# A two-layer encoder on one core: mask and maximum in one instruction, scaled queries, one sine product per rotation, a new TensorE order, first weights in halves

## The chip, the cores and the metric

The kernel runs on one core of a Trainium2 chip. The metric is the device time of one execution in microseconds; lower is better. The core has five engines that run their own instruction streams and wait for each other by semaphores: TensorE (PE in the profile; PEld is its weight load), VectorE (DVE), ScalarE (ACT), GpSimd (POOL) and SyncE (SP), which here does nothing but start DMA transfers. TensorE writes its results to PSUM, from where ACT and DVE take them.

## The reference

Input is x of 256 tokens by 1024, float32. There are two layers (DEPTH 2), each of three parts with a layer norm behind it:

```
x = layer_norm(ALPHA * x + 0.5 * swiglu(x, ffn1_w_in[l], ffn1_w_out[l]), ...)
mix = hybrid_mixer(x, cos, sin, mask, w_in[l], w_out[l], ...)
x = layer_norm(ALPHA * x + mix, ...)
x = layer_norm(ALPHA * x + 0.5 * swiglu(x, ffn2_w_in[l], ffn2_w_out[l]), ...)
```

`swiglu` is (silu(x Wg) * (x Wu)) W_out with a hidden width of 2816. The mixer projects x by one matrix into dq, dk, dv (512 columns each, 4 heads of two 64-wide halves), sq (512, 8 heads), sk and sv (128 each, 2 heads). The q and k parts are rotated (`t * cos + rot * sin`, where rot swaps the halves of each 64 columns and negates one). The first group is a differential attention, softmax(q1 k1) - lam * softmax(q2 k2), scores times 1/8, with a root-mean-square norm of each head. The second is attention in a window of 128 to either side, with a sink per head:

```
m = jnp.maximum(jnp.max(s, axis=-1, keepdims=True), sk)
e = jnp.exp(s - m)
p = e / (jnp.sum(e, axis=-1, keepdims=True) + jnp.exp(sk - m))
```

Both outputs side by side go through one output projection.

## The kernel before, in words

Every matrix product that needs float32 accuracy is made of three: a weight tile `raw` (128 by 1024 float32, 512 KB, by a DMA that SP starts) is split into `wh`, a cast on ACT (line 79), and `wl`, the rest, a subtraction on DVE (line 80). The activations lie in `xx`, hi and lo, transposed. A product is then hi x wh, hi x wl and lo x wh. There are 317 casts in all: 316 tiles, the first of them in two halves. `Weights._make` makes a tile, `get(i)` asks for tiles up to 8 ahead. `raw` has 5 buffers, `wh` and `wl` 9 each, so a cast can wait for the matmuls that used the buffer before. ACT and DVE are in-order: a cast that waits holds all behind it.

TensorE's order is the order in which the program is written (`manual_schedule`). The order on ACT, DVE and SP is made by a scheduler from priorities and its own estimate of times; `tc.high_priority` puts work ahead, and the splitting of weights stands 100 behind (`LATER`).

An FFN has a first part of 1024 columns, all 8 blocks k of the contraction for both token halves (`first`, tile `hb`, line 308), then 18 column tiles (`col`, tiles `hg` and `hu`, lines 340 and 342), then the second matrix (`step`, tile `acc`, line 390). The first FFN begins the program: its xx comes from `x_tr` by `load_xt`, in pieces of k (0:1, 1:2, 2:4, ...), between the first weight tiles. Nine matmuls on zeros (`wps`, line 162) run before the first real one.

The mixer is a list of steps, ORDER, for token blocks t of 128: `P nm t c` does c of the four parts of projection nm (tile `pj`, lines 455 to 457) and behind the last the rotation `rope_` on DVE (lines 470, 473, and 477 or 479); `X` transposes the second block of x; `T` transposes a rotated q or k (tile `tq`); `S d q` and `S s q` are the scores of two heads for query block q (tiles `sd` and `ss`, line 497) with the softmax on DVE and ACT; `A` transposes weights of the differential attention (`tpd`, line 570), `V` multiplies them by v (`od`) and normalises to `y`; `W` does the same for the windowed part (`tps`, `os`, line 614); `Y` transposes y into xx; `O t c` does c of the eight steps of the output projection (tile `ao`, line 678); `G` loads a norm's factors; `Z` transposes x for what follows.

In `swa_scores` a unit of two heads has two score tiles of 128 by 2 by 256. The mask is added to one half of each (line 539), the maximum is taken (line 540), line 543 scales it and takes the maximum with the sink, lines 546 and 547 make the arguments of exp, then follow the exps on ACT (line 554), sums, reciprocals and four multiplications (line 562).

Of the kernel before, what the change touches and what calls it, by code (L numbers as in the profile page):

```python
# [9 lines left out]
F32 = mybir.dt.float32  # L10
# [36 lines left out]
ORDER = """  # L47
P dk 0 1; P dq 0 2; P dk 0 2; X; P dq 0 1; P dq 1 1; P dk 0 1; P dv 0 2; P dk 1 2; P dq 0 1; P dv 1 1; P dq 1 2;
P dk 1 2; P dv 1 2; P dq 1 1; P dv 0 1; P dv 1 1; T dk 1; T dk 0; T dq 0; P sk 0 1; P dv 0 1; S d 0; P sq 0 1; T
dq 1; P sk 1 1; S d 0; P sk 0 1; P sk 1 3; P sq 0 1; A 0 0; T sk 1; P sk 0 1; S d 1; S d 1; P sk 0 1; P sq 0 2;  # L50
P sq 1 2; A 0 1; T sq 0; T sk 0; V 0; S s 0; P sq 1 1; A 1 1; A 1 0; P sq 1 1; S s 0; V 1; Y 0; G; T sq 1; O 0
2; S s 1; W 0 0; O 0 1; Y 1; W 0 1; W 0 2; O 0 1; S s 1; O 1 1; W 1 0; O 0 1; O 1 1; O 0 1; W 1 1; O 0 2; W 1 2;
O 1 4; Z; O 1 2
"""
# [38 lines left out]
def encoder_kernel(  # L93
# [84 lines left out]
    def load_x():  # L178
        for t in range(2):
# [18 lines left out]
    inv_t = cp.tile([P, 32], F32, name="inv_t")  # L198
    cos_t = cp.tile([P, 2, HD], F32, name="cos_t")
    sin_t = cp.tile([P, 2, HD], F32, name="sin_t")  # L200

    def rotary():
# [43 lines left out]
        dv.tensor_scalar(a, a, -1.0, math.pi / 2, ALU.mult, ALU.add)  # L246
        nc.scalar.activation(sin_t[:, :, 32:64], r, AF.Sin)
        nc.scalar.activation(cos_t[:, :, 0:32], a, AF.Sin)
        dv.tensor_copy(cos_t[:, :, 32:64], cos_t[:, :, 0:32])
        dv.tensor_scalar(sin_t[:, :, 0:32], sin_t[:, :, 32:64], -1.0, None, ALU.mult)  # L250

# [43 lines left out]
    def ffn(l, n, last=False):  # L295
# [4 lines left out]
        def first(ts, mid=None):  # L300

            hp = [[ps.tile([P, 512], F32, tag="b", name=f"hb_{nm}_{t}{s}") for s in range(2)] for t in ts]
            for k in range(KT):
                wh, wl = W.get(wi + k)
                for t, hb in zip(ts, hp):
                    for g, ww, e in ((0, wh, 0), (0, wl, 1), (1, wh, 2)):
                        for s in range(2):
                            mm(hb[s], xx[:, k, g, t, :], ww[:, 512 * s : 512 * s + 512],  # L308
                               start=(k == 0 and e == 0), stop=(k == KT - 1 and e == 2))
                if k == KT - 3 and mid is not None:  # L310
                    mid()
# [110 lines left out]
    def mixer(l):  # L422
# [38 lines left out]
        def rope_(pt, nh, t, nm, perm=False):  # L461
# [6 lines left out]
            m2v = m2[:, 0:w].rearrange("p (h d) -> p h d", d=HD)  # L468
            c = cos_t[:, t : t + 1, :].to_broadcast([P, nh, HD])
# [348 lines left out]
```

## Time and profile before

| what | value |
|---|---|
| median of three runs | 964.08 us (963.94 to 964.37) |
| the profiled execution's own time | 964.06 us |
| its span, first to last instruction | 962.2 us |
| PE busy | 947.0 us (98%) |
| DVE busy | 673.7 us (70%) |
| ACT busy | 509.4 us (53%) |
| mean granted TensorE clock | 0.997 |

The profile comes from one execution. Its own time is its span and about 1.9 us around it. Busy time of PE counts a matmul up to its modelled end, so matmuls overlap in the rows: a 128x512 matmul is shown with about 390 ns, while the next one starts after about 227. A wait of less than the overlap leaves no idle time in the rows, so start times say more than idle times.

### The profile page before, as it was taken

What the parts mean: (1) busy time and instruction counts of PE and PEld (TensorE: products, weight loads), DVE (VectorE), ACT (ScalarE), POOL (GpSimd) and SP (SyncE); (2) the same over time, 40 slices, a digit from 0 to 9 for tenths busy, and PEclk for the clock granted to TensorE, in tenths of its full rate; (3) what the DMA queues carried; (4) which work ended last, traced back from release to release, by engine and by line L of the source; (5) the groups of instructions that cost most, each with busy time, mean ns of one, the idle gap of its engine ahead of it and who ended that gap; (6) DMA issues with size and microseconds to landing.
All of it is one profiled execution on the core that took longest, in us unless ns stands there. A gap on an engine that the chain in (4) does not pass through costs nothing.

```text
span 962.2 us, 13695 instructions
## 1 busy us (share of the span) xinstructions
PE 947.0 (98%) x5087; PEld 801.8 (83%) x5087; DVE 673.7 (70%) x1099; ACT 509.4 (53%) x887; POOL 16.9 (2%) x27
## 2 busy tenths in 40 slices
PE   8999999999999999999999999999999999999997
PEld 6888888888778888888888888888887788888886
DVE  6887754589968776664587667547898787667534
ACT  5668553336755656543346555433576556555420
POOL 0000000000000000000000000000000000000000
PEclk9999999999999999999999999999999999999999
DMA  8886555366415755556376555563752276555511
GB/s 314 301 288 195 185 185 194 123 221 198 131 47 176 267 191 191 183 185 193 123 252 230 196 179 194 179 195 127 259 137 90 75 234 239 196 178 196 177 64 44
DMA packets 50946, 176.42 MB, mean 183 GB/s; under 512 B 6208, under 2 KB 8000, under 8 KB 50880
## 3 DMA queue, kind: packets, MB, share of 16 engines
q1 hardware_dynamic: 50880, 175.55, 55.6%
q8 instruction: 40, 0.66, 0.3%
q14 instruction: 26, 0.21, 0.1%
HBM read 174.48 MB, written 1.05 MB: 182 GB/s over the span
## 4 chain that ended last, share of the span: by engine, by line
PE 91%; DVE 5%; ACT 1%; issue 1%; DMA 0%; POOL 0%; SPq 0%; DVEq 0%; ACTq 0%
PE acc L390 25%; PE hg L340 14%; PE hu L340 14%; PE hb L308 9%; PE hu L342 7%; PE hg L342 7%; PE ao L678 4%; DVE wl L80 1%; PE tps L570 1%; PE os L614 1%; PE pj_dq L457 1%; PE pj_dv L457 1%; PE pj_dq L455 1%; PE pj_dv L456 1%; PE pj_dk L457 1%; PE pj_dv L455 1%
## 5 line engine op out<-in xcount | busy, mean ns | idle before, releaser
L80 DVE TENSOR_TENSOR wl<-raw,wh 128x1024 fp32r<-128x1024 f32 (+1 forms) x317 | 385.5, 1219 | 206.7 <-ACT wh L79 204.0
L79 ACT CAST wh<-raw 128x1024 fp32r<-128x1024 f32 (+1 forms) x317 | 332.1, 1050 | 330.7 <-PE acc L390 123.7
L390 PE MATMUL acc<-wh,g 128*128 128x512 f32 (+1 forms) x748 | 192.7, 377 | 0.0
L390 PEld LDWEIGHTS acc<-wh,g 128*128 128x128 f32 x748 | 136.0, 188 | 25.8
L340 PE MATMUL hg<-xx,wh 128*128 128x512 f32 x576 | 144.8, 393 | 0.0
L340 PE MATMUL hu<-xx,wh 128*128 128x512 f32 x576 | 144.2, 392 | 0.0
L340 PEld LDWEIGHTS hg<-xx,wh 128*128 128x128 f32 x576 | 103.6, 189 | 18.6
L340 PEld LDWEIGHTS hu<-xx,wh 128*128 128x128 f32 x576 | 103.6, 189 | 18.5
L390 PE MATMUL acc<-wl,g 128*128 128x512 f32 (+1 forms) x374 | 111.4, 377 | 0.0
L342 PEld LDWEIGHTS hg<-xx,wl 128*128 128x128 f32 x576 | 78.6, 190 | 5.7
L342 PEld LDWEIGHTS hu<-xx,wl 128*128 128x128 f32 x576 | 78.6, 190 | 5.6
L342 PE MATMUL hu<-xx,wl 128*128 128x256 f32 x576 | 80.3, 282 | 0.0
L342 PE MATMUL hg<-xx,wl 128*128 128x256 f32 x576 | 80.3, 282 | 0.0
L390 PEld LDWEIGHTS acc<-wl,g 128*128 128x128 f32 x374 | 68.9, 188 | 13.2
L308 PE MATMUL hb<-wh,xx 128*128 128x512 f32 x256 | 71.1, 395 | 1.0 <-ACT wh L79 1.0
L308 PEld LDWEIGHTS hb<-wh,xx 128*128 128x128 f32 x256 | 48.5, 191 | 11.7 <-ACT wh L79 1.8
L308 PE MATMUL hb<-wl,xx 128*128 128x512 f32 x128 | 40.4, 396 | 0.8 <-DVE wl L80 0.8
L678 PE MATMUL ao<-wh,xx 128*128 128x512 f32 x128 | 39.0, 406 | 1.8 <-DVE xx L270 1.0
L347 DVE TENSOR_TENSOR tl<-tl 128x256 f32<-128x256 f32 x72 | 30.6, 425 | 2.6 <-ACT tl L345 0.4
L349 ACT CAST g<-tl 128x256 fp32r<-128x256 f32 x72 | 28.9, 402 | 6.2 <-DVE tl L347 6.2
L350 DVE TENSOR_TENSOR g<-tl,g 128x256 fp32r<-128x256 f32 x72 | 30.1, 419 | 1.9 <-ACT g L349 1.9
L678 PEld LDWEIGHTS ao<-wh,xx 128*128 128x128 f32 x128 | 22.6, 188 | 9.6 <-issue 2.3
(182 smaller groups left out, 950.3 us busy)
## 6 DMA issues: line engine op xcount, KB each, us to landing
raw<-in_f_in_dram SPq DMA_DIRECT2D x144, 512.0 KB, 3.7
raw<-in_f_out_dram SPq DMA_DIRECT2D x88, 512.0 KB, 3.5
raw<-in_m_in_dram SPq DMA_DIRECT2D x36, 512.0 KB, 4.0
raw<-in_f_b_dram SPq DMA_DIRECT2D x31, 512.0 KB, 3.5
raw<-in_m_out_dram SPq DMA_DIRECT2D x8, 512.0 KB, 4.9
raw<-in_m_out_dram SPq DMA_DIRECT2D x16, 256.0 KB, 4.5
lng<-in_ln_g_dram SPq DMA_DIRECT2D x6, 512.0 KB, 5.5
lnb<-in_ln_b_dram SPq DMA_DIRECT2D x6, 512.0 KB, 6.1
```

What stands on the lines that cost most here:

```text
L79: nc.scalar.copy(wh[:, s], raw[:, s])
L80: nc.vector.tensor_tensor(wl[:, s], raw[:, s], wh[:, s].bitcast(F32), ALU.subtract)
L308: mm(hb[s], xx[:, k, g, t, :], ww[:, 512 * s : 512 * s + 512], start=(k == 0 and e == 0), stop=(k == KT - 1 and e == 2))
L340: mm(hs[s], wh[:, k * P : (k + 1) * P], xx[:, k], start=(k == 0), stop=False)
L342: mm(hs[s][:, 1, :], wl[:, k * P : (k + 1) * P], xx[:, k, 0], start=False, stop=(k == KT - 1))
L347: dv.tensor_tensor(gv, tl[:, 0], gv, ALU.mult)
L349: nc.scalar.copy(gs[q][:, jj, 0, :], gv)
L350: dv.tensor_tensor(gs[q][:, jj, 1, :], gv, gs[q][:, jj, 0, :].bitcast(F32), ALU.subtract)
L390: mm(a, g, ww[:, s], start=(k == 0 and e == 0), stop=(k == JT - 1 and e == 2))
L455: mm(o, xx[:, k, 0, t, :], wh[:, s], start=(k == 0), stop=False)
L457: mm(o, xx[:, k, 1, t, :], wh[:, s], start=False, stop=(k == KT - 1))
L678: mm(acc[t][h], xx[:, k, g, t, :], ww[:, s], start=(k == 0 and e == 0), stop=(k == KT - 1 and e == 2))
```

## The change

Five edits.

- First weights: the first three tiles (before: the first one) are loaded, cast and subtracted in halves of 512 columns, and without the lower priority; the first piece of x_tr is started by ACT in place of SP; for k below 3 the matmuls go by halves s, hi x wh for both token blocks, then lo x wh, then hi x wl.
- Mask and maximum: the mask is three blocks wide (a triangle, zeros, the other triangle), and one DVE instruction per head row of 256 adds it, starts the maximum from the sink and writes both. The lines that added the mask to halves, reduced and took the maximum with the sink are gone.
- Scale: cos and sin exist twice, one copy times 1/8, which the queries use. The exps lose their scale, the differential maximum is negated in the reduction, and its own multiplication by -1/8 goes.
- Rotation: one product with the sine over all 64 columns, reading the halves in reversed order, in place of two.
- The list ORDER is another one, and the scratch tile `jk` has one buffer in place of two.

```diff
-P dk 0 1; P dq 0 2; P dk 0 2; X; P dq 0 1; P dq 1 1; P dk 0 1; P dv 0 2; P dk 1 2; P dq 0 1; P dv 1 1; P dq 1 2;
+P dq 0 3; P dk 0 2; P dq 0 1; P dk 0 1; X; P dk 0 1; P dq 1 1; P dv 1 1; P dv 0 1; P dk 1 1; P dv 0 1; P dv 1 1;
...
-        n = 512 if i == 0 else 1024
+        n = 512 if i < 3 else 1024
...
-            with self.tc.high_priority(-LATER):
+            with self.tc.high_priority(0 if i < 3 else -LATER):
...
-        nc.sync.dma_start(xr, x_tr[:, :, k, :])
+        (nc.sync if k0 else nc.scalar).dma_start(xr, x_tr[:, :, k, :])
...
+        for tab in (cos_t, sin_t):
+            dv.tensor_scalar(tab[:, 0], tab[:, 1], SCALE, None, ALU.mult)
...
+                parts = ((0, wh, 0), (0, wl, 1), (1, wh, 2))
+                if wi + k < 3:
+                    todo = [(t, hb, parts[e], s) for s in range(2) for e in (0, 2, 1) for t, hb in zip(ts, hp)]
+                else:
+                    todo = [(t, hb, p, s) for t, hb in zip(ts, hp) for p in parts for s in range(2)]
...
-            for h in range(2):
-                sn = sin_t[:, t : t + 1, 32 * h : 32 * h + 32].to_broadcast([P, nh, 32])
-                dv.tensor_tensor(m2v[:, :, 32 * h : 32 * h + 32], src[:, :, 32 - 32 * h : 64 - 32 * h], sn, ALU.mult)
+            sn = sin_t[:, tab, t : t + 1, :].to_broadcast([P, nh, HD]).rearrange("p h (x d) -> p h x d", x=2)
+            dv.tensor_tensor(m2v.rearrange("p h (x d) -> p h x d", x=2),
+                             src.rearrange("p h (x d) -> p h x d", x=2)[:, :, ::-1, :], sn, ALU.mult)
...
-                    dv.tensor_reduce(mx[:, 2 * c : 2 * c + 2], sc[c], AX.X, ALU.max)
-                dv.tensor_scalar(mx, mx, -SCALE, None, ALU.mult)
+                    dv.tensor_reduce(mx[:, 2 * c : 2 * c + 2], sc[c], AX.X, ALU.max, negate=True)
...
-                    mb = mask[:, qt : qt + 1, :].to_broadcast([P, 2, P])
-                    dv.tensor_tensor(sc[v][:, :, ob], sc[v][:, :, ob], mb, ALU.add)
-                    dv.tensor_reduce(mx[:, 2 * v : 2 * v + 2], sc[v], AX.X, ALU.max)
+                    for i in range(2):
+                        q = 2 * v + i
+                        dv.tensor_tensor_reduce(sc[v][:, i, :], sc[v][:, i, :], mask[:, (1 - qt) * P : (3 - qt) * P], 1.0, sk[:, v, i : i + 1],
+                                                ALU.add, ALU.max, mx[:, q : q + 1])
...
-                dv.scalar_tensor_tensor(mx2, mx2, SCALE, sk, ALU.mult, ALU.max)
```

How the instructions stand. TensorE at the start, behind the nine matmuls on zeros, all twelve matmuls of the first k: before, where `hb_00` and `hb_01` are the two column halves of token block 0, `hb_10` and `hb_11` those of block 1, `wh_99` and `wl_100` the parts of the first tile:

```order
L308 MATMUL hb_00_195<-wh_99,xx 128x512
L308 MATMUL hb_01_196<-wh_99,xx 128x512
L308 MATMUL hb_00_195<-wl_100,xx 128x512
L308 MATMUL hb_01_196<-wl_100,xx 128x512
L308 MATMUL hb_00_195<-wh_99,xx 128x512
L308 MATMUL hb_01_196<-wh_99,xx 128x512
L308 MATMUL hb_10_197<-wh_99,xx 128x512
```

and now:

```order
L318 MATMUL hb_00_201<-wh_99,xx 128x512
L318 MATMUL hb_10_203<-wh_99,xx 128x512
L318 MATMUL hb_00_201<-wh_99,xx 128x512
L318 MATMUL hb_10_203<-wh_99,xx 128x512
L318 MATMUL hb_00_201<-wl_100,xx 128x512
L318 MATMUL hb_10_203<-wl_100,xx 128x512
L318 MATMUL hb_01_202<-wh_99,xx 128x512
```

The second matmul no longer needs the second half of the tile; `wl` is first read by the fifth in place of the third, the second half of `wh` by the seventh.

DVE in the first mixer around the rotation of sq for block 0 (`m_0_sq`, `r_sq`), which TensorE's `T sq 0` waits for; `ed` are weights of the differential attention, `wl` a weight tile's rest: before

```order
L524 SCALAR_TENSOR_TENSOR ed_2349<-ed_2349,wt_2357 128x256 x2
L80 TENSOR_TENSOR wl_2214<-raw_2212,wh_2213 128x1024
L470 TENSOR_TENSOR m_0_sq_2431<-pj_sq_2205,cos_t 128x512
L473 TENSOR_TENSOR m_0_sq_2432<-pj_sq_2205,sin_t 128x8x32 x2
L520 RECIPROCAL rd_2385<-dd_2380 128x4
L477 TENSOR_TENSOR r_sq_2433<-m_0_sq_2431,m_0_sq_2432 128x2x4x64
```

and now, up to the lo parts of sq and sk that `S s 0` needs (`sqT`, `skT`):

```order
L481 TENSOR_TENSOR m_0_sq_2418<-pj_sq_2281,cos_t 128x512
L484 TENSOR_TENSOR m_0_sq_2419<-pj_sq_2281,sin_t 128x512
L531 RECIPROCAL rd_2373<-dd_2368 128x4
L535 SCALAR_TENSOR_TENSOR ed_2338<-ed_2338,wt_2346 128x256
L489 TENSOR_TENSOR r_sq_2420<-m_0_sq_2418,m_0_sq_2419 128x2x4x64
L533 SCALAR_TENSOR_TENSOR wt_2375<-dd_2368,nlam_1867,rd_2373 128x2
L504 TENSOR_TENSOR skT_1875<-tq_sk_2438,skT_1875 128x128
L535 SCALAR_TENSOR_TENSOR ed_2367<-ed_2367,wt_2375 128x256 x2
L81 TENSOR_TENSOR wl_2284<-raw_2282,wh_2283 128x1024
L81 TENSOR_TENSOR wl_2297<-raw_2295,wh_2296 128x1024
L504 TENSOR_TENSOR sqT_1874<-tq_sq_2455,sqT_1873 128x4x128
L504 TENSOR_TENSOR skT_1875<-tq_sk_2462,skT_1875 128x128
```

The weight tile that stood ahead of the rotation now stands behind it, with another one, and both stand ahead of the lo parts.

TensorE in the first mixer from the second windowed scores to the third: before

```order
L678 MATMUL ao_2648<-wh_2122,xx 128x512
L678 MATMUL ao_2649<-wh_2122,xx 128x512
L678 MATMUL ao_2648<-wl_2123,xx 128x512
L678 MATMUL ao_2649<-wl_2123,xx 128x512
L678 MATMUL ao_2648<-wh_2122,xx 128x512
L678 MATMUL ao_2649<-wh_2122,xx 128x512
L497 MATMUL ss_2674<-skT_1867,sqT_1865 128x256 x2
L497 MATMUL ss_2674<-skT_1867,sqT_1866 128x256
```

and now, `V 1` having moved ahead of these scores:

```order
L688 MATMUL ao_2642<-wh_2149,xx 128x512
L688 MATMUL ao_2643<-wh_2149,xx 128x512
L688 MATMUL ao_2642<-wl_2150,xx 128x512
L688 MATMUL ao_2643<-wl_2150,xx 128x512
L688 MATMUL ao_2642<-wh_2149,xx 128x512
L688 MATMUL ao_2643<-wh_2149,xx 128x512
L509 MATMUL ss_2680<-skT_1875,sqT_1873 128x256 x2
L509 MATMUL ss_2680<-skT_1875,sqT_1874 128x256
```

Three output steps (18 matmuls on `ao`) now stand between the transposes of sq and the scores that need them, where two stood.

## Rows read from the trace of the kernel before

**Rows 1.** the page's first part: busy us, share of span, instructions.

```profile
PE 947.0 (98%) x5087; PEld 801.8 (83%) x5087; DVE 673.7 (70%) x1099; ACT 509.4 (53%) x887; POOL 16.9 (2%) x27
```

**Rows 2.** timeline of the start: start us, us, what, [idle before].

```profile
0.73 0.68 SPq L167 DMA_DIRECT2D xr<-in_x_tr_dram  x1
...
1.18 3.41 PE L162 MATMUL wps<-wz 128*128 128x512 bf16 x9 [1.18 <-DVE wz L159]
...
1.47 1.05 SPq L77 DMA_DIRECT2D raw<-in_f_b_dram  x2
...
4.73 1.32 ACT L79 CAST wh<-raw 128x512 fp32r<-128x512 f32 x2 [2.51 <-DMA raw<-in_f_b_dram]
...
5.40 0.50 PE L308 MATMUL hb<-wh,xx 128*128 128x512 f32 x1 [0.81 <-ACT wh L79]
...
7.64 0.80 PE L308 MATMUL hb<-wl,xx 128*128 128x512 f32 x1 [0.81 <-DVE wl L80]
...
8.98 1.05 ACT L79 CAST wh<-raw 128x1024 fp32r<-128x1024 f32 x1 [2.94 <-DMA raw<-in_f_b_dram]
...
10.74 1.08 PE L308 MATMUL hb<-wh,xx 128*128 128x512 f32 x4
...
11.66 0.63 PE L308 MATMUL hb<-wl,xx 128*128 128x512 f32 x2
```

**Rows 3.** windows of the start: PE, PEld, DVE, ACT, POOL, clock, DMA.

```profile
4.60:7.64 3.04, 1.24 (x3) 0.48 (x3) 1.64 (x4) 1.24 (x2) 0.00 (x0) 0.93 0.86 222
7.64:10.40 2.76, 2.76 (x7) 2.18 (x8) 0.89 (x3) 1.05 (x1) 0.00 (x0) 0.50 1.03 358
10.40:20.00 9.60, 9.60 (x43) 7.98 (x42) 9.36 (x11) 6.27 (x6) 0.00 (x0) 0.99 1.02 400
```

**Rows 4.** timeline of PE in the first mixer.

```profile
246.34 0.60 PE L570 MATMUL tpd<-ident,ed 128*128 128x128 f32 x4
247.75 0.63 PE L489 MATMUL tq_sq<-ident,r_sq 128*128 128x128 f32 x4 [0.80 <-DVE wt L522]
248.21 0.27 PE L489 MATMUL tq_sk<-ident,r_sk 128*128 128x128 f32 x1
...
258.07 0.60 PE L267 MATMUL tr_y<-ident,y 128*128 128x128 f32 x4
258.66 0.66 PE L489 MATMUL tq_sq<-ident,r_sq 128*128 128x128 f32 x4
259.67 0.73 PE L678 MATMUL ao<-wh,xx 128*128 128x512 f32 x2 [0.35 <-ACT xx L269]
...
263.45 0.50 PE L497 MATMUL ss<-skT,sqT 64*128 64x256 f32 x2
264.75 0.98 PE L497 MATMUL ss<-skT,sqT 64*128 64x256 f32 x10 [0.80 <-DVE sqT L492]
265.65 1.09 PE L570 MATMUL tps<-ident,esw 128*128 128x128 f32 x8
...
268.48 1.30 PE L570 MATMUL tps<-ident,esw 128*128 128x128 f32 x8
269.70 1.95 PE L614 MATMUL os<-pTs,vs 128*64 128x256 f32 x16
```

**Rows 5.** waits of PE: us in total, times, longest.

```profile
PE tq_sq L489 <- DVE wt L522: 1.6, 2, 0.8
```

**Rows 6.** DVE by line, 225 to 300 us: count, busy, mean ns.

```profile
L80 DVE TENSOR_TENSOR wl<-raw,wh 128x1024 fp32r<-128x1024 f32 x15 | 18.2, 1216 | 0.0
L540 DVE TENSOR_REDUCE mxs<-ss 128x2 f32<-128x512 f32 x8 | 5.3, 683 | 0.0
...
L539 DVE TENSOR_TENSOR ss<-ss,mask 128x256 f32<-128x256 f32 x8 | 3.2, 425 | 0.0
...
L492 DVE TENSOR_TENSOR sqT<-tq_sq,sqT 128x512 fp32r<-128x512 f32 x2 | 1.3, 670 | 0.0
...
L543 DVE SCALAR_TENSOR_TENSOR mxs<-mxs,snk 128x4 f32<-128x4 f32 x4 | 0.6, 156 | 0.0
```

More of the change, by code (lines that the diff above doesn't have):

```diff
@@ L47 @@
 ORDER = """
-P dk 0 1; P dq 0 2; P dk 0 2; X; P dq 0 1; P dq 1 1; P dk 0 1; P dv 0 2; P dk 1 2; P dq 0 1; P dv 1 1; P dq 1 2;
[L49 to L53, printed above, removed]
+P dq 0 3; P dk 0 2; P dq 0 1; P dk 0 1; X; P dk 0 1; P dq 1 1; P dv 1 1; P dv 0 1; P dk 1 1; P dv 0 1; P dv 1 1;
+P dk 1 1; P dq 1 1; P dk 1 1; P dv 1 1; P dk 1 1; P dq 1 1; P dv 0 1; P dv 1 1; T dk 0; T dq 0; T dk 1; P sk 1
+1; P sk 0 1; P dq 1 1; P dv 0 1; S d 0; S d 0; P sk 0 1; T dq 1; P sk 0 1; P sk 1 2; P sq 0 2; P sk 1 1; S d 1;
+S d 1; P sk 0 1; P sq 0 2; A 0 1; A 0 0; T sk 1; P sq 1 2; T sq 0; T sk 0; V 0; A 1 0; S s 0; P sq 1 1; A 1 1; P
+sq 1 1; G; V 1; S s 0; Y 0; T sq 1; O 0 3; S s 1; O 0 1; W 0 0; Y 1; S s 1; W 0 1; W 0 2; O 1 1; W 1 0; O 0 2; O
+1 1; O 0 2; W 1 1; W 1 2; O 1 4; Z; O 1 2
 """
@@ L186, in encoder_kernel @@
     make_identity(nc, ident)
-    mask = cp.tile([P, 2, P], F32, name="mask")
+    mask = cp.tile([P, 3, P], F32, name="mask")
     nc.gpsimd.memset(mask, 0.0)
+    nc.gpsimd.affine_select(out=mask[:, 2, :], in_=mask[:, 2, :], compare_op=ALU.is_ge, fill=NEG,
+                            base=0, pattern=[[-1, P]], channel_multiplier=1)
     nc.gpsimd.affine_select(out=mask[:, 0, :], in_=mask[:, 0, :], compare_op=ALU.is_ge, fill=NEG,
-                            base=0, pattern=[[-1, P]], channel_multiplier=1)
-    nc.gpsimd.affine_select(out=mask[:, 1, :], in_=mask[:, 1, :], compare_op=ALU.is_ge, fill=NEG,
                             base=0, pattern=[[1, P]], channel_multiplier=-1)
+    mask = mask.rearrange("p a b -> p (a b)")
     mhalf = cp.tile([P, 4], F32, name="mhalf")
@@ L198, in encoder_kernel @@
     inv_t = cp.tile([P, 32], F32, name="inv_t")
-    cos_t = cp.tile([P, 2, HD], F32, name="cos_t")
-    sin_t = cp.tile([P, 2, HD], F32, name="sin_t")
+    cos_t = cp.tile([P, 2, 2, HD], F32, name="cos_t")
+    sin_t = cp.tile([P, 2, 2, HD], F32, name="sin_t")
     def rotary():
@@ L246, in rotary @@
         dv.tensor_scalar(a, a, -1.0, math.pi / 2, ALU.mult, ALU.add)
[L247 to L250, printed above, removed]
+        nc.scalar.activation(sin_t[:, 1, :, 32:64], r, AF.Sin)
+        nc.scalar.activation(cos_t[:, 1, :, 0:32], a, AF.Sin)
+        dv.tensor_copy(cos_t[:, 1, :, 32:64], cos_t[:, 1, :, 0:32])
+        dv.tensor_scalar(sin_t[:, 1, :, 0:32], sin_t[:, 1, :, 32:64], -1.0, None, ALU.mult)
+        for tab in (cos_t, sin_t):
+            dv.tensor_scalar(tab[:, 0], tab[:, 1], SCALE, None, ALU.mult)
     def load_gb(l, n):
@@ L304, in first @@
                 wh, wl = W.get(wi + k)
[L305 to L309, printed above, removed]
+                parts = ((0, wh, 0), (0, wl, 1), (1, wh, 2))
[3 more added lines that the diff above has]
+                    todo = [(t, hb, p, s) for t, hb in zip(ts, hp) for p in parts for s in range(2)]
+                for t, hb, (g, ww, e), s in todo:
+                    mm(hb[s], xx[:, k, g, t, :], ww[:, 512 * s : 512 * s + 512],
+                       start=(k == 0 and e == 0), stop=(k == KT - 1 and e == 2))
                 if k == KT - 3 and mid is not None:
@@ L468, in rope_ @@
             m2v = m2[:, 0:w].rearrange("p (h d) -> p h d", d=HD)
-            c = cos_t[:, t : t + 1, :].to_broadcast([P, nh, HD])
+            tab = int(nm[-1] == "k")
+            c = cos_t[:, tab, t : t + 1, :].to_broadcast([P, nh, HD])
             dv.tensor_tensor(m1v, src, c, ALU.mult)
-            for h in range(2):
-                sn = sin_t[:, t : t + 1, 32 * h : 32 * h + 32].to_broadcast([P, nh, 32])
-                dv.tensor_tensor(m2v[:, :, 32 * h : 32 * h + 32], src[:, :, 32 - 32 * h : 64 - 32 * h], sn, ALU.mult)
+            sn = sin_t[:, tab, t : t + 1, :].to_broadcast([P, nh, HD]).rearrange("p h (x d) -> p h x d", x=2)
+            dv.tensor_tensor(m2v.rearrange("p h (x d) -> p h x d", x=2),
+                             src.rearrange("p h (x d) -> p h x d", x=2)[:, :, ::-1, :], sn, ALU.mult)
             if perm:
@@ L516, in diff_scores @@
                         q = 2 * c + i
-                        nc.scalar.activation(e[:, c, i, :], sc[c][:, i, :], AF.Exp, bias=mx[:, q : q + 1], scale=SCALE,
+                        nc.scalar.activation(e[:, c, i, :], sc[c][:, i, :], AF.Exp, bias=mx[:, q : q + 1],
                                              accum_out=den[:, q : q + 1])
@@ L553, in swa_scores @@
                         q = 2 * v + i
-                        nc.scalar.activation(e[:, v, i, :], sc[v][:, i, :], AF.Exp, bias=mx[:, q : q + 1], scale=SCALE,
+                        nc.scalar.activation(e[:, v, i, :], sc[v][:, i, :], AF.Exp, bias=mx[:, q : q + 1],
                                              accum_out=den[:, q : q + 1])
@@ L588, in diff_pv @@
                         hd = 2 * u + i
-                        jk = tp.tile([P, P], F32, tag="jk", name=f"jk{l}{qt}{hd}", bufs=2)
+                        jk = tp.tile([P, P], F32, tag="jk", name=f"jk{l}{qt}{hd}", bufs=1)
                         nc.scalar.activation(jk, o[:, hd, :], AF.Square, scale=rc[:, i : i + 1], accum_out=sq[:, hd : hd + 1])
```

3 lines of the change are left out of this document (1 added, 2 removed).

## The prediction, made before the changed kernel was run

> **What bounds the kernel now.** I read the page's first part first. PE is busy 98% of the span, DVE 70%, ACT 53% [rows 1]. So work taken off DVE or ACT is worth nothing by itself, and time can only come from where PE waits. Its 2% idle understate that: a wait shorter than the modelled overlap of two matmuls leaves no idle time, so I compare start times with the spacing of the same kind elsewhere. Next came the timeline of the start and its windows [rows 2, 3]. Real matmuls begin at 5.40, go in bits up to 10.74, and only from there run without stops, four in 0.92 us, thus 0.23 each. In 4.60 to 7.64 PE is busy 1.24 of 3.04 us; in the next window its granted clock is 0.50, the lower level (1.2 GHz), and then 0.99 (2.4 GHz). Third, PE's timeline in the first mixer [rows 4] and its waits [rows 5]: there PE stands behind DVE and ACT in short pieces, the largest 0.80 us, and the wait of `tq_sq` is there in both layers.
>
> **The start.** Before, the first x_tr piece is issued by SP at 0.73 and takes 0.68 there, so the first half of tile 0 is issued at 1.47 only [rows 2]. Now ACT issues that piece and SP the weights at once, 0.74 earlier. If the transfer keeps its length, the first cast starts at 4.73 - 0.74 = 3.99 and takes 0.66 (1.32 for two), so `wh` stands at 4.65, just as the matmuls on zeros end (1.18 + 3.41 = 4.59). The next four matmuls need this half alone, the fifth needs `wl`, the seventh the second half. The twelve matmuls of k 0 take 2.7 us at 0.227 (2.4 GHz) or 5.1 us at twice that (1.2 GHz), and end at 7.4 to 9.8.
>
> Tile 1 is now two transfers of 262 KB. Its cast began at 8.98 behind a wait for the transfer of 2.94 [rows 2]. Its first half comes 0.7 earlier for the issue and some 0.9 earlier because the other half need not have landed (262 KB at 222 to 358 GB/s is 1.2 to 0.7 us [rows 3]): 7.4, and 8.05 with its cast. So k 1 begins between 8.05 and 9.8 in place of 10.74, a gain of 0.9 to 2.7. The low clock followed a stretch in which PE mostly waited; now PE waits little between 4.6 and 8, so I count on 2.4 GHz for most of it and take 2.3, less 0.3 for the `wl` of later tiles: **2.0**. The Trainium skill ("TensorE: Matmul & The Clock Gate", Part 1) says that the lower rate is the default which activity lifts, at a point that varies from run to run. By that the gain could lie anywhere between the two ends; no run here shows the variation.
>
> What halving costs: 1.32 us of casts in place of 1.05 for a tile, three times, on an ACT that was idle 2.94 ahead of the cast of tile 1 [rows 2]. The wait for the DMA hides it. If loads ran ahead, it would be 0.3 a tile.
>
> **The mixers' order.** From start to start in the first mixer [rows 4], less what the work needs by itself: `T sq 0` 1.41, four transposes 0.46 (247.75 to 248.21), late 0.95; `tr_y` 0.59 - 0.46 = 0.13; `T sq 1` 1.01 - 0.46 = 0.55; the two output steps 3.78 for twelve matmuls of 0.227, 1.06; `S s 1` 2.20 for twelve of 0.09 (ten from 264.75 to 265.65), 1.1; second `tps` 1.22 for eight, 0.3. The sum is 4.1 us a layer.
>
> In the new order the weight tile (1.22, line 80 [rows 6]) no longer stands ahead of the rotation of sq, which is more than the 0.95 that `T sq 0` lost; this wait goes. `S s 1` has a third output step ahead of it, 6 x 0.227 = 1.36 against 1.1; this goes too. What is late next: `S s 0`, as its lo parts (0.67 [rows 6]) now stand on DVE behind two `wl` of 1.22 and three multiplications, some 4.3 us of DVE work against 2.9 of PE and an estimated 0.8 by which DVE comes ahead into this stretch, so 0.6. `T sq 1`, 0.3. The first output step, 0.8: the cast of y into xx stands on ACT behind a weight cast of 1.05 and squares which now share one `jk` buffer. And the second transposes of the first `W`, 0.85, which want a PSUM slot that DVE empties late, behind mask and multiplications. These add to 2.55. The pairs of `S d` steps save one change between shapes of matmul, some 0.2. So 4.1 - 2.55 + 0.2 = **1.8 a layer**, 3.6 for two. The bounds: none of the new waits, 4.3 a layer; new waits as large as the old, 0.2. I take the sum, since the waits that go have rows and those that come are counted from instructions with rows.
>
> **Mask and maximum.** Before, a unit has two additions of 425 ns and two reductions of 683 [rows 6], 2.2 us with a small multiplication and maximum beside them. Now it has four instructions 256 wide, each with a read of the accumulator. No row shows the new one. The low bound is a simple addition of that width, 0.43 less the overlap of neighbours, about 0.34; the high one is an addition, half a reduction (0.34) and a read like the smallest operations (156 ns [rows 6]), together 0.93. I take 0.5, nearest to the addition: 4 x 0.5 = 2.0, even. The Trainium skill ("Vector Engine (DVE) Microarchitecture Reference", section 7) warns that a three-operand instruction with two SBUF sources wider than bf16 halves its throughput. Here one source is in PSUM, and no row shows such an instruction; by the rule it would add (683 - 425) = 258 ns to 425, 0.69 each.
>
> **The rest** I put at nothing: one sine product of full width in place of two of half of it (the full one estimated at the 0.67 of another 512-wide operation [rows 6]), the small multiplications that go (0.16), two small table products while the FFN runs. DVE is idle 30%, and PE covers it. Uncovered, each is under 0.4 us a layer, of either sign.
>
> **Sum.** The execution's own time of 964.06, which agrees with the median of 964.08: 964.06 - 2.0 - 3.6 = **958.5**.
>
> **Rivals.** (1) The order only moves waits: DVE and ACT have the same work in the same stretch, and PE is late as much elsewhere. For it speaks that the estimated waits already return 60% of what goes; against it that two weight tiles are plainly put behind the scores' path. Start gain alone: 964.06 - 2.0 = 962.1. (2) The start gains little: the clock stays at 1.2 GHz through k 0, or the transfer is no earlier because ACT's issue is late and both loads share the same DMA engines; the DMA share is already 0.86 in 4.60 to 7.64 [rows 3]. Start 0.9, mixers 3.6: 959.6. (3) Slower: the mask instruction with its read is dear. Each of the 32 that costs 0.93 in place of 0.49 adds 0.44; in three of the four units of a layer the transposes `tps` wait for DVE, so 24 x 0.44 = 10.6 and the time is 969.1. It decides from about 0.8 an instruction: (0.8 - 0.49) x 24 = 7.4 eats the gain of 5.6 and 0.2% above. For it: a separate read each time, and DVE behind the scores is already what PE waits for. Against it: the wide reduction alone is 0.68 for twice the width. (4) The new waits are mostly hidden by the modelled slack: start 2.3, mixers 3.0 each: 955.8.
>
> **Chances.** Forecast 0.58, rival 1 0.14, rival 2 0.12, rival 3 0.10, rival 4 0.06. A measurement of this kernel can tell 0.2%, or 1.9 us, from no change: under 962.1 is faster, over 966.0 slower. The forecast, rivals 2 and 4 and a third of rival 1 are faster, but for 0.03 on the edge of the forecast and 0.01 of rival 2: 0.77. The rest of rival 1 and these make 0.13. Rival 3 is 0.10. The range runs from rival 4 to a little above rival 1, 955.6 to 962.9; rival 3 and the outer edges, under 2 in 10, are left out.
>
> **What would show it.** The start: first real matmul at about 4.6, k 1 at 8 to 10, and a clock that is not 0.50 in between; if the first half-cast does not begin by 4.1, the DMA step is wrong. The mixer: `T sq 0` and `S s 1` follow the work ahead without a gap, and small gaps stand at `S s 0`, the first `ao` and the second `tps`. The mask line: 0.4 to 0.55 from one to the next; at 0.8 or more rival 3 has won. The prediction is wrong if the first mixer takes as long as before, or if a gap of over 1.5 us stands anywhere in it.

## The result and the profile after

The changed kernel takes 955.84 us (median of four runs, 955.55 to 956.16), the kernel before beside it 964.01 (963.86 to 964.37): a ratio of 0.9911 with a 95% interval of 0.9899 to 0.9923 (estimated over all runs; the two medians alone divide to 0.9915). It is 8.2 us faster where 5.5 were forecast, a time at the lower end of the range. The span fell from 962.2 to 954.0 us.

The page's first part, as in [rows 1]:

```profile
PE 942.0 (99%) x5087; PEld 801.7 (84%) x5087; DVE 669.2 (70%) x1103; ACT 510.4 (54%) x889; POOL 17.0 (2%) x27
```

PE has 5 us less of busy time and 3 us less of idle time. Its matmuls are the same 5087; one that starts after a stop or at the lower clock is shown longer (0.50 and 0.80 in [rows 2], against some 0.39), so fewer stops shorten the busy time too. DVE has 4.5 us less of busy time, ACT 1.0 more.

The timeline of the start, as in [rows 2], and the window of k 0 (PE, PEld, DVE, ACT, POOL, clock, DMA), as in [rows 3]:

```profile
0.73 0.62 ACTq L168 DMA_DIRECT2D xr<-in_x_tr_dram  x1
...
0.74 0.86 SPq L78 DMA_DIRECT2D raw<-in_f_b_dram  x2
...
4.16 0.62 ACT L80 CAST wh<-raw 128x512 fp32r<-128x512 f32 x1 [1.28 <-DMA raw<-in_f_b_dram]
4.54 0.29 DVE L170 CAST xx<-xr 128x256 fp32r<-128x256 f32 x1 [3.41 <-DMA xr<-in_x_tr_dram]
...
4.98 1.30 PE L318 MATMUL hb<-wh,xx 128*128 128x512 f32 x4
...
6.12 0.64 PE L318 MATMUL hb<-wl,xx 128*128 128x512 f32 x2
...
6.29 0.62 ACT L80 CAST wh<-raw 128x512 fp32r<-128x512 f32 x1 [0.42 <-DMA raw<-in_f_b_dram]
...
7.99 1.08 PE L318 MATMUL hb<-wh,xx 128*128 128x512 f32 x4
```

```profile
4.98:7.99 3.01, 3.01 (x14) 2.46 (x13) 2.66 (x6) 1.24 (x2) 0.00 (x0) 1.00 0.96 318
```

The first x_tr piece and the first weights leave at the same moment, and the first cast of weights starts at 4.16 (4.73 before). The x_tr piece, which now travels beside the weights, is ready later: its first cast starts at 4.54 (3.43 before). PE works from 4.98 to 7.99 without a stop, where before it was stopped by `wh` and `wl` and had a stretch at clock 0.50. The first matmul on `hg`, the next part, starts at 27.14 us; before it was 30.25. That is 3.1 us, and it stays at 3.1 up to the first mixer.

PE's timeline in the first mixer, as in [rows 4]:

```profile
243.13 0.39 PE L467 MATMUL pj_sq<-wh,xx 128*128 128x512 f32 x1
243.74 0.63 PE L501 MATMUL tq_sq<-ident,r_sq 128*128 128x128 f32 x4 [0.22 <-DVE wt L533]
...
246.63 0.38 PE L509 MATMUL ss<-skT,sqT 64*128 64x256 f32 x1
247.84 0.98 PE L509 MATMUL ss<-skT,sqT 64*128 64x256 f32 x11 [0.83 <-DVE skT L504]
...
254.87 0.66 PE L273 MATMUL tr_y<-ident,y 128*128 128x128 f32 x4
255.54 0.66 PE L501 MATMUL tq_sq<-ident,r_sq 128*128 128x128 f32 x4
256.71 0.72 PE L688 MATMUL ao<-wh,xx 128*128 128x512 f32 x2 [0.52 <-ACT xx L275]
...
261.04 0.98 PE L509 MATMUL ss<-skT,sqT 64*128 64x256 f32 x12
...
265.77 0.66 PE L580 MATMUL tps<-ident,esw 128*128 128x128 f32 x4
266.74 0.66 PE L580 MATMUL tps<-ident,esw 128*128 128x128 f32 x4 [0.30 <-DVE xx L276]
```

The wait at `T sq 0` has become 0.38 (0.61 from the matmul before, less the usual spacing of 0.23) and that ahead of the third windowed scores is gone (261.04). New is a wait of 1.1 in the first windowed scores (246.63 to 247.84, less 0.11); the first output step waits 0.7 (255.93, the last transpose, to 256.71, less 0.11); the second transposes of `W 0 1` wait 0.47. The first mixer lasts 101.18 us in place of 103.56, the second 101.12 in place of 103.72: 5.0 together. Start and mixers make up the 8.2 us (the rest, 0.1, lies at the end).

DVE by line, 225 to 297 us (count, busy us, mean ns), and the first and the next other instruction of one unit of mask and maximum in its timeline:

```profile
L551 DVE CUSTOM_DVE_ANT_0 ss<-ss,mask,snk 128x256 f32<-128x256 f32 x16 | 7.0, 486 | 0.0
...
L551 DVE DVE_READ_ACCUMULATOR2_ANT mxs<- 128x1 f32 x16 | 2.3, 141 | 0.0
```

```profile
263.04 0.49 DVE L551 CUSTOM_DVE_ANT_0 ss<-ss,mask,snk 128x256 f32<-128x256 f32 x1
...
264.66 0.35 DVE L572 TENSOR_SCALAR esw<-esw,rs 128x256 f32<-128x256 f32 x1
```

One instruction shows 486 ns, but the next starts 0.405 us after it, with the accumulator's read of 141 ns underneath: four take 1.62 us (263.04 to 264.66). Before, a unit took 1.94 (two additions 0.66, two reductions 1.20, the maximum 0.08, each by start times).

### The profile page after: what moved, and what is told of

Read it like the earlier page. It is cut to its first block, busy times and chain, and to the rows that moved or that the text cites. A ratio compares the mean times of both kernels' runs of the same rounds, so it can differ in the third digit from the quotient of the medians.

```text
span 954.0 us, 13703 instructions
## 1 busy us (share of the span) xinstructions
PE 942.0 (99%) x5087; PEld 801.7 (84%) x5087; DVE 669.2 (70%) x1103; ACT 510.4 (54%) x889; POOL 17.0 (2%) x27
## 4 chain that ended last, share of the span: by engine, by line
PE 90%; DVE 6%; ACT 2%; issue 1%; POOL 0%; DVEq 0%
PE acc L400 25%; PE hg L350 14%; PE hu L350 14%; PE hb L318 9%; PE hu L352 7%; PE hg L352 7%; PE ao L688 4%; DVE wl L81 1%; ACT ed L528 1%; PE os L624 1%; PE pj_dq L467 1%; PE pj_dq L466 1%; PE pj_dk L467 1%; PE pj_dq L465 1%; PE pj_dk L466 1%
## 5 line engine op out<-in xcount | busy, mean ns | idle before, releaser
L354 DVE TENSOR_TENSOR tl<-hu,tl 128x256 f32<-128x256 f32 x72 | 30.0, 417 | 2.8 <-ACT tl L353 2.8
```

The source lines that it names most:

```text
L354: dv.tensor_tensor(tl[:, s], hs[s][:, 0, :], tl[:, s], ALU.add)
```

## The experiments

Where a time by tile is given, it is the time from each matmul's start to the next one's, summed over all matmuls of a tile in one mixer; so a wait counts for the tile in front of it. Twelve runs follow, each timed beside the kernel before (medians of 964.1 to 964.3); behind each time stand its ratio to that and the 95% interval. First the parts alone.

**The start's edits alone** on the kernel before:

```diff
-        n = 512 if i == 0 else 1024
+        n = 512 if i < 3 else 1024
-            with self.tc.high_priority(-LATER):
+            with self.tc.high_priority(0 if i < 3 else -LATER):
-        nc.sync.dma_start(xr, x_tr[:, :, k, :])
+        (nc.sync if k0 else nc.scalar).dma_start(xr, x_tr[:, :, k, :])
...
```

> The kernel before with the start's edits alone (three tiles in halves, new order of their matmuls, first x_tr piece from ACT). Theory A (the gain of 8.2 us is 3.1 at the start and 5.0 in the two mixers, and the parts add): 960.9 us, first matmul on hb at about 5.0, k 1 at about 8.0. Rival B (what the start saves is lost again, since weights become the bound in the first FFN): 962.5 or more, with gaps of PE between 10 and 130 us.

Measured 961.29 us, ratio 0.9967 (0.9954 to 0.9980). The first matmul on `hg` is at 27.90, the mixers are as before (103.57, 103.72). Theory A holds in its time, and rival B falls; but k 1 starts at 8.86, where 8.0 was expected. The matmul on `hg` is 0.8 later than in the changed kernel with the same edits: here the first four matmuls of k 0 take 1.84 us (0.43 between two, like the matmuls on zeros before them), there 1.14. PE left the lower of its two clock levels (1.2 GHz) later. The Trainium skill ("TensorE: Matmul & The Clock Gate", Part 1) says that the point at which the clock rises varies from run to run. The traces agree: in the seven profiles with these edits the first four matmuls take 1.14 to 1.92 us, and `hg` begins at 27.1 to 27.9.

**Halves alone** (the edits above without the one of x_tr) and **the earlier issue alone** (only that one):

> The kernel before with the first three tiles in halves and the new order of their matmuls, x_tr still from SP. Theory D (the start gains through PE working without long stops on data that arrive in halves, which keeps the clock at 2.4 GHz; the earlier issue adds its 0.7): 961.6 us, k 1 at 8.7. Rival E (the earlier issue is what moves the start; halves alone leave the stops): 963.4 or more, and a stretch at clock 0.50 stays.

> The kernel before with only the first x_tr piece started by ACT. Theory D: the first matmul 0.4 to 0.7 earlier, the stops and the stretch at clock 0.50 stay, 963.4 us. Rival E: 962 or less.

Halves: 961.63 us, 0.9973 (0.9963 to 0.9983), `hg` at 27.86, k 1 at 8.21, and from the first matmul on no stretch under clock 1.00: theory D's time to 0.1 us, with k 1 0.5 earlier than it said. Issue: 962.98, 0.9989 (0.9980 to 0.9998), `hg` at 29.09, a gain of 1.2 in the trace where 0.7 was expected; here too the clock stayed at 1.00 past 7 us, which theory D did not expect. The two do not add: by the traces 2.4 and 1.2 alone, 2.4 to 3.1 together.

**PE kept busy in the stops of k 0**, with no transfer or cast moved:

```diff
-WARM = 9
+WARM = 11
...
+FILL = {(0, 0): 2, (1, 0): 4}
...
+                            if wi + k == 0 and t == 0 and (e, s) in FILL:
+                                for _ in range(FILL[e, s]):
+                                    mm(wps, wz[:, 0:P], wz, start=True, stop=True)
```

> The kernel before with eight more matmuls on zeros: two more ahead of the first weights, two and four in the stops between the first matmuls of k 0, so that PE is busy while it waits. No load or cast moves. Theory D, clock part (in the kernel before eight matmuls of k 0 went at 1.2 GHz, 0.2 us more each): k 1 at 9.6 to 10.1 in place of 11.19, 962.7 us. Rival F (data bound k 1, the clock cost nothing): 964.0, k 1 at 11.

Measured 964.36 us, 0.9999 (0.9990 to 1.0007). Its timeline of the second tile and the window from k 1 to k 2:

```profile
9.05 1.05 ACT L82 CAST wh<-raw 128x1024 fp32r<-128x1024 f32 x1 [3.08 <-DMA raw<-in_f_b_dram]
...
9.80 1.10 PE L311 MATMUL hb<-wh,xx 128*128 128x512 f32 x4
10.13 1.22 DVE L83 TENSOR_TENSOR wl<-raw,wh 128x1024 fp32r<-128x1024 f32 x1
...
11.41 0.73 PE L311 MATMUL hb<-wl,xx 128*128 128x512 f32 x2 [0.51 <-DVE wl L83]
```

```profile
10.27:13.81 3.54, 3.03 (x13) 2.17 (x13) 3.40 (x5) 2.11 (x2) 0.00 (x0) 1.00 1.00 368
```

The clock is 1.00 throughout, k 1 starts at 10.27 in place of 11.19, and then its `wl` matmuls wait for tile 1, cast at 9.05 and subtracted from 10.13 to 11.35. The next part starts at 30.13, 0.1 earlier. Rival F holds in its time: some eight matmuls at half the clock cost about 1.6 us of PE in the kernel before, but tile 1, loaded whole, bound the start just as closely. The halves remove both bounds.

**The order alone** (the new ORDER in the kernel before):

> The kernel before with the new list ORDER alone. Theory A (the order carries the mixers' gain, the DVE edits nothing): 959.0 us, each mixer 101.1 to 101.3 us in place of 103.6. Rival C (the order pays only with the shorter DVE work): 961.5 or more, a mixer of 102.4 or longer, with PE waits at the windowed scores or the transposes of their weights that are 0.5 us longer than in the changed kernel.

Measured 961.80 us, 0.9977 (0.9968 to 0.9986); mixers 102.32 and 102.15, a gain of 2.8 together. PE's longest wait:

```profile
PE tps L570 <- DVE esw L562: 2.5, 4, 1.1
```

Rival C holds (its mixers of 102.4 or more missed by 0.1 and 0.3): the waits at the windowed scores are gone (3.65 us of `ss` in place of 5.25), but the transposes of their weights (`tps`) take 5.55 us in place of 3.95: PE runs into the softmax.

**All DVE edits alone** (the changed kernel with the old ORDER and the old start):

> The changed kernel with the old ORDER and the old start: mask and maximum, scale, rotation and the single jk buffer alone. Theory A: 963.5 to 964.3 us, PE's waits where they were. Rival C (DVE's work on the scores' path is part of the mixers' gain): 961.5, the waits of the first mixer at T sq 0 and S s 1 shorter by 0.5 us each.

Measured 970.80 us, 1.0066 (1.0052 to 1.0081), its six runs from 968.26 to 972.78: slower than before, which neither theory had. PE's waits, the windows of the start and of the first mixer, and PE there:

```profile
PE tps L576 <- DVE es L552: 3.2, 2, 1.6
PE ss L505 <- DVE skT L500: 2.6, 2, 1.3
```

```profile
12.00:16.00 4.00, 3.47 (x9) 2.79 (x10) 3.80 (x6) 2.57 (x3) 0.00 (x0) 0.64 1.04 410
...
252.00:256.00 4.00, 2.72 (x20) 2.08 (x19) 2.62 (x9) 1.83 (x8) 1.02 (x1) 0.93 0.80 274
256.00:260.00 4.00, 4.00 (x17) 3.41 (x16) 3.89 (x15) 2.47 (x5) 0.00 (x0) 0.64 0.27 111
```

```profile
253.97 0.98 PE L505 MATMUL ss<-skT,sqT 64*128 64x256 f32 x11 [1.28 <-DVE skT L500]
```

Of the 7.8 us that the span grew, 2.6 lie at the start (`hg` at 32.87). There PE waits 1.8 for a `wl`, and the clock is at its lower level at about 13 to 16.5; the kernel before, with the same loads and the same order of PE, has such a fall at 7.6 to 10.4 [rows 3]. Whether the DVE edits have a part in that was not separated. The other 5.2 are the mixers, which last 105.99 and 106.52. Waits of 1.3 us at the scores and 1.6 at `tps` replace those of 0.8. In the first mixer the granted clock falls behind the wait at the scores: in 252 to 260 the shortfall is (0.07 + 0.36) x 4 = 1.7 us of work. In the second it falls behind the wait at `tps`, with as much in 744 to 752 (0.87 and 0.71). So up to 3.4 of the 5.2 are clock.

**The same with the old mask lines back:**

```diff
...
-                        dv.tensor_tensor_reduce(sc[v][:, i, :], ...)
...
+                    dv.tensor_tensor(sc[v][:, :, ob], sc[v][:, :, ob], mb, ALU.add)
+                    dv.tensor_reduce(mx[:, 2 * v : 2 * v + 2], sc[v], AX.X, ALU.max)
...
+                dv.tensor_tensor(mx2, mx2, sk, ALU.max)
```

> The run e3 (old ORDER, old start, all DVE edits) with the old mask lines put back: what stays of the change is the rotation, the scale and the single jk buffer. Theory K (the new mask instruction moves the scheduler's order of DVE in the old ORDER so that PE's waits come close together and the clock falls): 963.7 to 964.5, mixers 103.5, no stretch of the mixers under clock 1.00. Rival L (the single jk buffer or the rotation does it): 967 or more, the clock falls in the mixers as in e3.

Measured 966.74 us, 1.0032 (1.0019 to 1.0044): between the two. The mixers last 104.67 and 104.91, 1.1 and 1.2 longer than before, mostly at the windowed scores (`ss` 6.58 us in place of 5.25):

```profile
PE ss L505 <- DVE skT L500: 2.6, 2, 1.3
PE ss L505 <- DVE sqT L500: 1.6, 2, 0.8
```

```profile
252.20 0.98 PE L505 MATMUL ss<-skT,sqT 64*128 64x256 f32 x11 [1.28 <-DVE skT L500]
```

In this profile the clock stays at 1.00 in the mixers, as theory K says, but that the falls of the run before came with the mask instruction is not shown. The wait of 1.28 at the scores, behind which the clock fell in the first mixer there, is here too, and no fall follows it; only the wait of 1.6 at `tps` went with the mask instruction. And two of the nine runs took 969.71 and 970.15 at a mean clock of 0.995 over the whole run, the others 966.34 to 967.24 at 0.996 to 0.998.

As for the longer wait at the scores, rotation, scale or the single `jk`, none of which adds work to DVE in the mixers, moved DVE's order against the old ORDER. Which of the three was not separated.

**The changed kernel with the old mask lines** (the same edit, in the new ORDER and start):

> The changed kernel with the old mask lines (two additions to halves, two reductions, one maximum with the sink) in place of the four new instructions. In the trace of the changed kernel these follow each other every 0.405 us, 1.62 a unit; before it was 0.34 + 0.60 a tile and 0.07, 1.95 a unit. Theory G (the new instruction shortens the way from scores to weights, and in the new order PE waits for that way): 958 us, mixers 102.0 to 102.4 as in the run with the order alone, the longer waits at the transposes of the windowed weights. Rival H (another DVE edit, or the scheduler's order alone, makes the difference of 1.1 a mixer): under 956.5.

Measured 959.43 us, 0.9947 (0.9935 to 0.9960); mixers 102.64 and 102.59. PE's waits:

```profile
PE tps L581 <- DVE esw L573: 1.4, 2, 0.7
PE tps L581 <- ACT pTs L583: 1.3, 2, 0.7
```

Theory G holds, with a time 1.4 above its 958 us: the mixers are 0.2 over its upper end, and the start is 0.8 later than in the changed kernel, as in the first run above. `tps` takes 5.66 us in place of 4.17 and all else is the same to 0.1: the mask instruction is worth 1.5 us a mixer in the new order, 2.9 together. That is more than three units at 1.94 - 1.62 = 0.32 ahead of the transposes; how much of the rest is a changed order on DVE stays open.

**The changed kernel with two sine products:**

```diff
...
+            for h in range(2):
+                sn = sin_t[:, tab, t : t + 1, 32 * h : 32 * h + 32].to_broadcast([P, nh, 32])
+                dv.tensor_tensor(m2v[:, :, 32 * h : 32 * h + 32], src[:, :, 32 - 32 * h : 64 - 32 * h], sn, ALU.mult)
```

> The changed kernel with two sine products of half the width in place of one. Theory G: 955.8 us within 0.5, mixers 101.1. Rival H: 957 or more, the waits at T sq and S s longer.

Measured 955.66 us, 0.9907 (0.9892 to 0.9922): theory G in its time; this version and the changed kernel are the fastest here and by their times cannot be told apart. But its mixers last 100.78 each, 0.4 and 0.3 less than in the changed kernel, where in five profiles with the mixers of the kernel before the same mixer differs by 0.1 at most. PE's wait at `T sq 0` is gone. The start of this profile is 0.5 later (`hg` at 27.60), which hides it in the time. So the single sine product gains nothing and by the traces costs some 0.3 a mixer. The product itself is no longer (one of 0.68 us against two of 0.41 that overlap); but DVE's order is another, and `r_sq`, which `T sq 0` waits for, begins 0.6 later, counted from the mixer's start.

**Three tries to fill the remaining waits**, each the changed kernel with steps of ORDER moved (shown are these steps alone, their lines joined; the first line is that of the changed kernel). `P sq` ahead of the waiting scores; the same with `Y 0` ahead of the next scores; and only `A 1 1` ahead of the waiting scores:

```diff
-A 1 0; S s 0; P sq 1 1; A 1 1; P sq 1 1; G; V 1; S s 0; Y 0; T sq 1;
+A 1 0; P sq 1 1; S s 0; A 1 1; P sq 1 1; G; V 1; S s 0; Y 0; T sq 1;
```

```diff
+A 1 0; P sq 1 1; S s 0; A 1 1; P sq 1 1; G; V 1; Y 0; S s 0; T sq 1;
```

```diff
+A 1 0; A 1 1; S s 0; P sq 1 1; P sq 1 1; G; V 1; S s 0; Y 0; T sq 1;
```

> The changed kernel with one step of ORDER moved: P sq 1 1 (1.36 us of matmuls) ahead of the first S s 0, where PE waits 1.1 us for the lo parts of sq and sk behind two weight tiles on DVE. Theory I (the wait is a matter of distance on PE, and nothing else is late for it): the wait goes, 0.9 a mixer, 954.0 us. Rival J (the time comes back as a wait at the next stage, since DVE's queue is what is full there): 955.5 or more.

> As the run before, and Y 0 ahead of the second S s 0, so that its cast and its lo part stand earlier than the first output step. Theory I: PE's wait at the first output step falls from 0.7 to 0.2, 953.2 us. Rival J: y of block 0 is not ready, PE waits at its transposes instead, 954.5 or more.

> The changed kernel with A 1 1 (four transposes, 0.44 us) ahead of the first S s 0 in place of behind the next P sq. DVE's order keeps nearly its rows, but the last part of y of block 0 moves behind two products of the rotation. Theory I (PE's wait at S s 0 can be filled as long as DVE's order stays): that wait falls from 1.1 to 0.7 and two switches go, 955.0 us. Rival J (y is late, PE waits at its transposes, as when P sq was moved): 957 or more, tr_y 1.0 us longer a mixer.

Measured 961.88 us (0.9974, 0.9964 to 0.9984), 960.98 (0.9961, 0.9948 to 0.9973) and 956.76 (0.9918, 0.9905 to 0.9930). Rival J holds in all three, in the third at another place than it named and a little under its figure. In the first, PE in the mixer, then DVE there, then the windows:

```profile
253.60 0.44 PE L273 MATMUL tr_y<-ident,y 128*128 128x128 f32 x2
254.44 0.33 PE L273 MATMUL tr_y<-ident,y 128*128 128x128 f32 x1 [0.40 <-DVE y L606]
255.30 0.33 PE L273 MATMUL tr_y<-ident,y 128*128 128x128 f32 x1 [0.53 <-DVE y L606]
...
257.21 0.79 PE L688 MATMUL ao<-wh,xx 128*128 128x512 f32 x2 [1.15 <-ACT xx L275]
```

```profile
252.44 0.35 DVE L606 SCALAR_TENSOR_TENSOR y<-od,f,gsb 128x128 f32<-128x128 f32 x1
...
252.78 0.68 DVE L481 TENSOR_TENSOR m_sq<-pj_sq,cos_t 128x512 f32<-128x512 f32 x1
253.38 0.68 DVE L484 TENSOR_TENSOR m_sq<-pj_sq,sin_t 128x512 f32<-128x512 f32 x1
...
254.04 0.34 DVE L606 SCALAR_TENSOR_TENSOR y<-od,f,gsb 128x128 f32<-128x128 f32 x1
254.30 0.68 DVE L489 TENSOR_TENSOR r_sq<-m_sq,m_sq 128x512 f32<-128x512 f32 x1
254.90 0.34 DVE L606 SCALAR_TENSOR_TENSOR y<-od,f,gsb 128x128 f32<-128x128 f32 x1
```

```profile
252.00:256.00 4.00, 3.07 (x27) 2.21 (x26) 4.00 (x13) 2.09 (x11) 0.00 (x0) 1.00 0.01 3
256.00:260.00 4.00, 2.85 (x9) 2.20 (x9) 3.33 (x16) 2.45 (x10) 1.01 (x1) 0.72 0.42 137
260.00:264.00 4.00, 4.00 (x24) 3.02 (x22) 2.76 (x9) 2.14 (x9) 0.00 (x0) 0.85 0.14 28
```

The wait at the scores is gone (`ss` 3.66 in place of 4.85), but `P sq` done earlier calls its rotation earlier, and the scheduler puts these products between the four parts of `y`. The transposes of `y` wait for each part, the cast behind them is late, the first output step waits 1.15, and behind these waits the clock falls to its lower level: (0.28 + 0.15) x 4 = 1.7 us of work. `tr_y` takes 1.2 more, `ao` 2.3, `tps` 0.7; the mixer is 3.5 longer. In the second run y is not ready either: `tr_y` takes 3.60 in place of 1.20, and the clock falls in both mixers as well. In the third, PE and then ACT, with one row of ACT in the changed kernel for comparison below:

```profile
248.27 0.98 PE L509 MATMUL ss<-skT,sqT 64*128 64x256 f32 x11 [0.39 <-DVE skT L504]
...
257.52 0.73 PE L688 MATMUL ao<-wh,xx 128*128 128x512 f32 x2 [1.59 <-ACT xx L275]
```

```profile
252.77 0.47 ACT L564 ACTIVATE esw<-ss,mxs 128x256 f32<-128x256 f32 x1
...
254.59 1.06 ACT L80 CAST wh<-raw 128x1024 fp32r<-128x1024 f32 x1
...
256.89 0.58 ACT L275 CAST xx<-tr_y 128x512 fp32r<-128x512 f32 x1
```

```profile
256.09 0.57 ACT L275 CAST xx<-tr_y 128x512 fp32r<-128x512 f32 x1
```

The scores wait 0.4 less, and PE comes to the transposes of y 0.5 earlier. But on ACT four exps, a weight cast and three squares stand ahead of the cast of y, as they do in the changed kernel, and they do not come earlier: counted from the mixer's start the cast of y is 0.4 later. So the first output step waits 1.59 in place of 0.52, and a mixer is 0.3 longer. The time is 0.9 above that of the changed kernel; the two mixers make 0.7 of the 1.1 by which the span is longer, a start 0.4 later the rest.

Summed by tile, first mixer, us:

| tile | before | order alone | changed, old mask | changed | P sq moved |
|---|---|---|---|---|---|
| ss | 5.25 | 3.65 | 4.86 | 4.85 | 3.66 |
| tps | 3.95 | 5.55 | 5.66 | 4.17 | 4.85 |
| tpd | 2.63 | 2.08 | 1.76 | 1.76 | 1.64 |
| tr_y | 1.09 | 1.02 | 1.23 | 1.20 | 2.39 |
| ao | 24.06 | 23.33 | 22.64 | 22.70 | 25.00 |
| all | 103.56 | 102.32 | 102.64 | 101.18 | 104.67 |

## Why the prediction was right and wrong

By terms, in us: forecast were 2.0 for the start, 3.6 for the order and nothing for mask and maximum; measured were 3.1, some 2.1 (the two mixers with the old mask lines), 2.9 (the new lines in their place) and 0.1 at the end.

**The start, forecast 2.0, measured 3.1.** The main step held: halves let PE work through k 0 without a stop. Two steps were off. The first cast came at 4.16, not 3.99, past the 4.1 that the prediction named as the sign of a wrong DMA step: the weights were 0.57 earlier in place of 0.74, and the x_tr piece beside them was ready 1.1 later than before, so the first real matmul stood at 4.98 and not at about 4.6. And that k 1 began at 7.99, close to the early end of 8.05, is luck: 8.05 was the first cast of tile 1, which in the trace was done at 6.91 (6.29 + 0.62), and what ended at 7.99 were the twelve matmuls of k 0. The size failed in three places. The base was misread: of the four matmuls in the row at 10.74 [rows 2] the first two still belong to k 0 (twelve to a k, counted from 5.40), so k 1 began at 11.19, 0.45 later. From a gain of 0.9 to 2.7 a value of 2.3 was taken, though the stretch without waits that the prediction itself described led to its end, 0.4 more. And 0.3 for later `wl` was 0.1. (A slip without effect: 5.1 us for twelve matmuls at the lower clock is right by the spacing of 0.425 between 8.24 and 9.94 in the kernel before, but is not twice 2.7.) The reason given for the size, the clock, was half of it: filling the stops kept the clock and gained 0.1, because tile 1 was a second bound of the same height.

**The order, forecast 1.8 a mixer; with all edits 2.4 and 2.6 were measured.** The forecast took mask and maximum as even, so what its term stands for is the run with the old mask lines: 0.9 and 1.1. By that the term was nearly twice too large, and the mixers' sum of 3.6 comes nearer to the 5.0 measured than its two terms come to theirs: two misses of opposite sign. The old waits that were to go went, but for 0.4 at `T sq 0`, and that went with two sine products. The new ones are 0.38 there, 1.1 at the scores (0.6 forecast), 0.2 at `T sq 1` (0.3), 0.7 at the first output step (0.8) and 0.47 at the second transposes (0.85): 2.85 against 2.55 forecast. With the old mask lines `tps` took 1.5 more, so that the wait put at 0.85 was then some 2.0. Far too small was also the gain by fewer switches between kinds of matmul: the forecast counted 0.2 for one pair. `ao` stands in six runs in place of eight, `os` and `sd` in two in place of three, and a change costs about 0.1 on entry (the first `ao` matmul 0.335 in place of 0.227) and 0.1 on leaving, an estimated 0.8 for the four. Then 4.1 - 2.85 + 0.8 = 2.05 of the 2.4 are accounted for; the rest is open.

**Mask and maximum, forecast nothing: the step that failed.** The duration was nearly right (0.405 us an instruction, forecast 0.5, bounds 0.34 and 0.93). Wrong was the term "even", and the premise at the head of the prediction that work taken off DVE is worth nothing by itself. A unit became 0.32 shorter, and in the new order PE waits for just this path: putting the old lines back cost 2.9 us in the two mixers. The prediction knew the path: its slower rival priced 24 of the 32 instructions as being on it. The same count with 0.49 - 0.405 gives 2.0 us of gain. A path that is exposed when an instruction is dear is exposed when it is cheap. The Trainium skill ("Vector Engine (DVE) Microarchitecture Reference", section 7) says that the scalar-tensor-tensor form with two non-bf16 SBUF sources halves throughput. By that rule the prediction reckoned 425 + 258 ns, which is 0.68 and not 0.69 us. Here one source is in PSUM, and the 256 columns took 0.405 from start to start, so no halving is seen.

**The rest**, put at nothing: the rotation by one sine product costs some 0.3 a mixer by the traces, within the 0.4 of either sign that the prediction allowed; scale and `jk` were not tried alone.

**The rivals.** That the order only moves waits is half true: with the old mask lines in otherwise the changed kernel, a mixer gains 0.9 to 1.1, and where single steps were moved further, every wait removed came back larger. The dear mask instruction did not come. The better case (955.8) hits the time by luck: the new waits are not hidden, they are longer than forecast, the start gained 3.1 in place of its 2.3, and the mixers 2.5 in place of its 3.0. The prediction's signs in the mixer came out as named, but for the 0.38 at `T sq 0`: small gaps at `S s 0`, the first `ao` and the second `tps`, none over 1.5, and 0.405 from one mask instruction to the next.

**The parts do not add.** In the two mixers the order alone gains 2.8, the DVE edits alone lose 5.2 on the old order, and both gain 5.0. Each program gets its own order on DVE and ACT from the scheduler, and in three of the programs the clock falls behind waits on top (3.4 us of the 5.2).

## What to carry to other kernels

Price a shorter instruction by the path it stands on: if its being longer would delay the busiest engine, its being shorter speeds it up. Where a planner orders the other engines, a step moved by hand moves their queues too: look where a removed wait comes out before counting it. Two bounds of equal height, here the clock and the load of tile 1, show as one in the profile; taking one away gained 0.1 us.

## What the runs showed of the hardware

The granted clock of PE fell to the lower of its two levels (1.2 GHz) in the middle of a busy kernel, in three of the programs and twice in each. With `P sq` moved it is 0.72 and 0.85 in two windows of 4 us, behind waits of 0.40, 0.53 and 1.15 us; in the changed kernel, whose waits in this stretch are 0.83 and 0.52 us and further apart, it stays at 1.00. Each fall took some 1.7 us of work, more than the 1.2 by which the scores' time had shrunk. The waits alone do not decide it: behind the same wait of 1.28 us the clock fell in the run with all DVE edits and not in the one with the old mask lines back, and it did not fall behind the single 1.59 of the third try. What does is open.

An instruction with an accumulated maximum and its separate read cost 0.405 us from start to start at 256 columns, less than the two rows of the profile, 486 and 141 ns, suggest: the read lies under the next instruction.
